# New prices in a planner: product times as traced, one transfer rate for all stages, and a short time for products with 32 stationary columns

## The chip, the cores and the metric

The kernel runs on one core of one Trainium2 chip. The metric is device time in microseconds (us) of one execution. The core has five engines that each work through their own instructions in a fixed order and wait for each other by semaphores: TensorE (PE, matrix products and transposes), VectorE (DVE), ScalarE (ACT), GpSimd (POOL) and SyncE (SP, which here only issues transfers). POOL issues transfers too. All transfers share 16 DMA engines.

## The reference

Two networks follow each other on 256 tokens of width 1024. The first has four layers, each a mixer and a SwiGLU FFN of width 2816; the mixers are a forgetting attention ("fox"), an S5 layer, a pooling layer, and fox again. The second has two layers with a hybrid mixer (retention, latent attention, mLSTM); the first has an FFN of width 2816, the second a mixture of 8 experts of width 3584, of which each token takes two.

```python
def first_block(x, ...):
    for i in range(DEPTH):                       # 4
        h = rms_norm(x, mix_norm_g[i])
        kind, j = i % N_MIXERS, i // N_MIXERS
        if kind == 0:   mix = forgetting_attention(h, fox_w_in[j], fox_b_f[j], fox_w_out[j])
        elif kind == 1: mix = s5_layer(h, s5_w_in[j], ...)
        else:           mix = multiscale_pool(h, pool_w[j], ...)
        x = x + mix
        x = x + swiglu(rms_norm(x, ffn_norm_g[i]), ffn_w_gate_up[i], ffn_w_down[i])
    return rms_norm(x, final_norm_g)

def second_block(x, ...):
    for l in range(DEPTH_2):                     # 2
        mix = hybrid_mixer(x, ...)
        x = layer_norm(DN_ALPHA * x + mix, ln1_w[l], ln1_b[l])
        f = swiglu_2(x, ...) if l % 2 == 0 else moe_swiglu(x, ...)
        x = layer_norm(DN_ALPHA * x + f, ln2_w[l], ln2_b[l])
    return x
```

The S5 layer computes u = h @ w_in, runs a complex linear recurrence over the 256 positions for each of 64 groups of 16 channels, and passes the result through a gated product with w_glu.

## The kernel before

**Products.** All is fp32. A product with a weight matrix is done with three products of a shorter type (fp32r): each weight tile of 128 rows and up to 1024 columns is loaded into a `raw` tile, ACT rounds it to `hi` (or scales and rounds it), DVE computes the rest `lo` (the split), and the activations have the same two parts `xh` and `xl`. The three are hi with xh, lo with xh, hi with xl, each in pieces of 512 columns: PE rows like `ps<-hi,xh`. The weight is loaded as the moving side, 512 columns at a time; the stationary side is the transposed activation of 128 tokens. There are 9 `raw` tiles (four of them are used by the S5 preparation until it ends) and 8 pairs of `hi` and `lo`. SP issues the weight loads, at most as far ahead as `raw` tiles are free.

**Stages.** An FFN goes through its width in blocks of 512 columns of gate and up, the last one of 256. Within a block all products of the first 128 tokens (t=0) come first, then those of t=1. At the end of each, ACT takes the silu of the gate and DVE multiplies it with up; the tail (`tail` in `ffn`) then transposes the result on PE, four 128x128 transposes (`ps<-ident,blk`, line L344), for the products with the down matrix.

**The S5 layer.** `s5_prep` computes the layer's tables (E, rot, T, G) from its parameters. It is started at the beginning and runs on DVE, ACT and PE between the other work of the first fox layer and its FFN. It loads the parameters in two halves with small loads on SP (`in_s_b_re`, `in_s_b_im`, `in_s_c_re`, `in_s_c_im`), and writes the tables to HBM by POOL. `s5` starts with `load`, which fetches the tables back, by POOL, as blocks of 128x512: 20 blocks ahead where the preparation has been planned to its end by then, else 11. The input product `gemm` comes next on PE; its result is scaled with the norm's rstd. In `rstd` a small product with a permutation matrix (loaded from `in_steps`) puts the two rstd vectors into the order of the layer (`ps<-rstd,blk`); the evacuation of the input product (`evac_u`) waits for that. rstd itself ends with a power on POOL (`rstd<-rstd,mhalf`), one for each 128 tokens. Four cores (`core(b)`) then do 16 products of 32 stationary columns each with the E table, the recurrence on DVE, and products with the T and G tables.

**What sets the order.** The class `Net` is a planner that runs while the program is built. It keeps a clock and a planned end for each engine, for the transfers and for each tile. Each piece of side work (a tail, the S5 preparation, a core, a norm) is a generator that sleeps until the planned time at which its data are there; `until` runs all generators that are due before the next product is put down. So the planned times decide where in PE's row each transposition or small product stands, and with it the order on the other engines. On the chip each engine then keeps that order, whatever the real times are. Products are priced in `mm` (L334 to L339), those of the MoE part with 64 stationary columns in `mm_cols` (L331), transposes in `tr` (L344, 0.107 us). Transfers are priced by their bytes over `rate`; `moe` sets `rate` to 395e3 (bytes per us) for its own stage already. An issue on POOL is planned at 1.04 us. Where the planner sees PE wait for 1.2 us or more, `reach` puts filler products of the identity with itself there (L287, planned at 0.214 us each); in the trace each is two rows.

Line L102 is the wrapper through which all instructions of DVE, ACT, POOL and SP pass, so their rows have that line.

Of the kernel before, what the change touches and what calls it, by code (L numbers as in the profile page):

```python
# [11 lines left out]
F32R = mybir.dt.float32r  # L12
# [103 lines left out]
class Net:  # L116
# [1 line left out]
    KEEP = 8  # L118
    BLK = 33
    AHEAD = 2.0  # L120
    rate = 358e3
    HYB = "ambr"
    BW = 528

# [208 lines left out]
    def mm(self, out, lhsT, rhs, start=True, stop=True):  # L333
        n = 1  # L334
        for d in rhs.shape[1:]:
            n *= d
        c = max(n * 0.4219, 107) / 1e3 if lhsT.dtype == F32R else max(n * 1.667, 214) / 1e3
        self.pe(out, (lhsT, rhs), c)
        self.nc.tensor.matmul(out, lhsT, rhs, start=start, stop=stop)  # L339

# [2416 lines left out]
```

## Time and profile before

| | us |
|---|---|
| three runs | 2611.97, 2620.14, 2619.58 |
| median | 2619.58 |
| the profiled execution | 2619.74 |
| its span in the trace | 2617.9 |
| PE busy | 2548.8 |
| mean granted clock of PE | 0.992 |

The trace times below count from the start of the span. The stages are, in us: first fox layer to 147, its FFN to 364, S5 layer from there to about 455, then the FFN of the S5 layer, the pooling layer, its FFN, the second fox layer and its FFN to about 1190, the two hybrid layers with an FFN between them to 1700, and the MoE part to the end. In a timeline a row can stand for several like instructions (x2, x4); its first number is the start of the first, the second the time from there to the end of the last, and a bracket gives the idle time of the engine before it and what ended it. Rows of products overlap, since a product is counted from its entry to its end.

### The profile page before, as it was taken

To read this page: it belongs to the slowest core of one execution; us is meant where nothing else is said; L and a number is where in the kernel's file an instruction comes from. 1 tells how busy PE (TensorE), PEld (TensorE's weight loads), DVE (VectorE), ACT (ScalarE), POOL (GpSimd) and SP (SyncE) were. 2 spreads that over 40 slices of the span, in tenths; PEclk is the share of its full clock that TensorE was granted. 3 is DMA by queue.
4 is the path that set the end of the run, shared out by engine and by line. 5 is a ranking of instruction groups with operands and counts; after the bars stand their busy time and mean duration, and the time that the engine had idled before them with its cause. 6 is when DMAs were issued, how large, how long until landed. Compare 5 with 4: busy or idle time off the path is not lost. (4 is left out here: it accounts for less than half of the span.)

```text
span 2617.9 us, 37366 instructions
## 1 busy us (share of the span) xinstructions
PE 2548.8 (97%) x12588; PEld 1959.1 (75%) x12588; DVE 1719.0 (66%) x2714; ACT 1294.3 (49%) x1829; POOL 130.7 (5%) x222
## 2 busy tenths in 40 slices
PE   8999999999999999999999999999999999999997
PEld 7887776788887888888878878886378883588852
DVE  6798776555655567556785467895088971498921
ACT  5644433454345455443644436484077760487820
POOL 2001034000000000000010010100000000000000
PEclk9999999999999999999999999999999999999999
DMA  6546778556355444564355643799999989999997
GB/s 222 155 153 215 246 256 283 169 165 231 115 189 191 146 138 149 174 209 144 113 191 167 208 141 113 228 373 356 404 386 397 375 309 365 398 395 388 388 368 310
DMA packets 307958, 649.35 MB, mean 248 GB/s; under 512 B 56746, under 2 KB 70408, under 8 KB 307760
## 3 DMA queue, kind: packets, MB, share of 16 engines
q1 hardware_dynamic: 294928, 608.23, 65.9%
q0 software_dynamic: 12640, 38.58, 4.5%
q8 instruction: 101, 1.65, 0.3%
q14 instruction: 97, 0.79, 0.1%
q10 hardware_dynamic: 192, 0.08, 0.0%
HBM read 635.29 MB, written 15.68 MB: 249 GB/s over the span
## 5 line engine op out<-in xcount | busy, mean ns | idle before, releaser
L339 PE MATMUL ps<-hi,blk 128*128 128x512 f32 x3024 | 844.6, 396 | 3.2 <-ACT hi L102 2.8
L102 DVE TENSOR_TENSOR lo<-raw,hi 128x1024 fp32r<-128x1024 f32 (+2 forms) x498 | 565.0, 1158 | 184.2 <-ACT hi L102 174.4
L339 PEld LDWEIGHTS ps<-hi,blk 128*128 128x128 f32 x3024 | 563.8, 189 | 133.6 <-ACT hi L102 5.1
L102 ACT CAST hi<-raw 128x1024 fp32r<-128x1024 f32 (+2 forms) x498 | 487.8, 1000 | 255.0 <-PE ps L339 209.9
L339 PE MATMUL ps<-lo,blk 128*128 128x512 f32 x1512 | 478.9, 395 | 1.1 <-DVE lo L102 1.1
L339 PE MATMUL ps<-lo,xh 128*128 128x512 f32 (+2 forms) x1296 | 418.5, 390 | 2.6 <-DVE lo L102 2.6
L339 PE MATMUL ps<-hi,xh 128*128 128x512 f32 (+2 forms) x1296 | 419.6, 390 | 1.0 <-ACT xh L102 0.9
L339 PE MATMUL ps<-hi,xl 128*128 128x512 f32 (+2 forms) x1296 | 417.7, 389 | 1.0 <-DVE xl L102 1.0
L102 DVE SCALAR_TENSOR_TENSOR lo<-raw,gam,hi 128x1024 fp32r<-128x1024 f32 (+3 forms) x272 | 303.0, 1134 | 81.1 <-ACT hi L102 69.3
L339 PEld LDWEIGHTS ps<-lo,blk 128*128 128x128 f32 x1512 | 282.8, 188 | 64.7 <-DVE lo L102 2.4
L102 ACT ACTIVATE hi<-raw,gam 128x1024 fp32r<-128x1024 f32 (+3 forms) x272 | 275.8, 1031 | 92.9 <-PE ps L339 73.6
L102 DVE TENSOR_TENSOR blk<-ps,blk 128x512 f32<-128x512 f32 (+4 forms) x220 | 139.5, 640 | 273.4 <-PE ps L331 140.7
L339 PEld LDWEIGHTS ps<-hi,xl 128*128 128x128 f32 x1296 | 241.1, 188 | 48.7 <-DVE xl L102 2.0
L339 PEld LDWEIGHTS ps<-lo,xh 128*128 128x128 f32 x1296 | 239.3, 189 | 50.2 <-DVE lo L102 4.7
L339 PEld LDWEIGHTS ps<-hi,xh 128*128 128x128 f32 x1296 | 239.5, 189 | 48.5 <-issue 2.2
L344 PE MATMUL ps<-ident,blk 128*128 128x128 f32 (+3 forms) x957 | 153.0, 278 | 16.1 <-DVE blk L102 12.8
L344 PEld LDWEIGHTS ps<-ident,blk 128*128 128x128 f32 (+3 forms) x957 | 110.6, 137 | 75.0 <-DVE blk L102 44.0
L102 ACT CAST blk<-ps 128x512 fp32r<-128x512 f32 (+2 forms) x137 | 76.2, 556 | 163.7 <-PE ps L344 109.7
L339 PE MATMUL ps<-blk 128*128 128x64 f32 (+11 forms) x1104 | 144.3, 304 | 5.2 <-DVE blk L102 3.1
L339 PEld LDWEIGHTS ps<-blk 128*128 128x128 f32 (+5 forms) x1104 | 118.7, 174 | 28.2 <-ACT blk L102 7.0
L102 ACT ACTIVATE blk<-ps 128x512 f32<-128x512 f32 (+1 forms) x75 | 41.8, 558 | 196.8 <-PE ps L331 135.4
L102 DVE TENSOR_TENSOR lo<-blk,hi 128x512 fp32r<-128x512 f32 x206 | 129.6, 683 | 0.5
(277 smaller groups left out, 1879.8 us busy)
## 6 DMA issues: line engine op xcount, KB each, us to landing
raw<-in_ffn_w_gate_up SPq DMA_DIRECT2D x320, 256.0 KB, 4.4
raw<-in_ffn_w_down SPq DMA_DIRECT2D x110, 512.0 KB, 4.9
raw<-in_moe_w_down SPq DMA_DIRECT2D x109, 512.0 KB, 7.0
raw<-in_moe_w_gate SPq DMA_DIRECT2D x101, 512.0 KB, 7.8
raw<-in_moe_w_up SPq DMA_DIRECT2D x99, 512.0 KB, 8.0
blk<-in_moe_w_up SPq DMA_DIRECT2D x98, 256.0 KB, 7.2
blk<-in_moe_w_gate SPq DMA_DIRECT2D x92, 256.0 KB, 7.8
blk<-in_moe_w_down SPq DMA_DIRECT2D x88, 256.0 KB, 6.6
```

Of the source, the lines that this page charges most:

```text
L102: return real(*a, **k)
L339: self.nc.tensor.matmul(out, lhsT, rhs, start=start, stop=stop)
L344: self.nc.tensor.transpose(out, in_, self.c["ident"][:p, :p])
```

## The change

Three constants of the planner change: the rate of transfers outside the MoE stage, the price of fp32r products (512 columns: 226.7 instead of 216.0 ns), and that of fp32 products (32 stationary columns with over 64 moving ones: 80 ns instead of 214 for 128 columns and 427 for 256; others 13.3 or 8 ns more). No product, split, load or wait is added or removed by hand; only the fillers change in number, from 152 to 157. Below the edit, all later lines have numbers higher by 6, so L339 is L345 and L344 is L350.

```diff
@@ class Net
-    rate = 358e3
+    rate = 395e3
@@ def mm
-        c = max(n * 0.4219, 107) / 1e3 if lhsT.dtype == F32R else max(n * 1.667, 214) / 1e3
+        if lhsT.dtype == F32R:
+            c = max(n * 0.4167 + 13.3, 113) / 1e3
+        elif lhsT.shape[-1] == 32 and n > 64:
+
+            c = 0.08
+        else:
+            c = max(n * 1.667 + 13.3, 222) / 1e3
         self.pe(out, (lhsT, rhs), c)
```

What the new prices do to the order is seen best at three places.

SP's queue in the first FFN, the kernel before: the 80 slices of the 512-wide blocks (gate and up of 8 weight tiles for each of five blocks), then those of the 256-wide block, with the S5 layer's small loads between them.

```order
L102 DMA raw<-in_ffn_w_gate_up 128x512 x80
L102 DMA raw<-in_ffn_w_gate_up 128x256 x10
L102 DMA blk<-in_s_b_re 64x32x16 x2
L102 DMA blk<-in_s_b_im 64x32x16 x2
L102 DMA blk<-in_s_c_re 128x4x64
L102 DMA blk<-in_s_c_im 128x4x64 x2
L102 DMA blk<-in_s_c_re 128x4x64
L102 DMA raw<-in_ffn_w_gate_up 128x256 x6
```

The same place on SP in the changed kernel.

```order
L102 DMA raw<-in_ffn_w_gate_up 128x512 x74
L102 DMA blk<-in_s_b_re 64x32x16 x2
L102 DMA blk<-in_s_b_im 64x32x16 x2
L102 DMA blk<-in_s_c_re 128x4x64
L102 DMA blk<-in_s_c_im 128x4x64 x2
L102 DMA blk<-in_s_c_re 128x4x64
L102 DMA raw<-in_ffn_w_gate_up 128x512 x6
L102 DMA raw<-in_ffn_w_gate_up 128x256 x16
```

The small loads stood ahead of the last six slices of the 256-wide block, and now stand ahead of the last six of the block before it. The preparation's last transposes move on PE from the S5 input product into the first FFN, 129 weight products earlier.

POOL between the end of the S5 preparation and the second norm's power, the kernel before; `s5E<-blk` and the like write tables to HBM, `blk<-s5E` and the like fetch them, and the two `rstd` rows are the powers of the first and the second 128 tokens.

```order
L102 TENSOR_TENSOR rstd_3486<-rstd_3486,mhalf 128x1
L102 DMA s5E<-blk 128x512
L102 DMA blk<-in_steps 128x512
L102 DMA blk<-s5E 128x512 x4
L102 DMA blk<-s5rot 64x512 x4
L102 DMA blk<-s5T 128x512 x4
L102 DMA s5E<-blk 128x512
L102 TENSOR_TENSOR rstd_3663<-rstd_3663,mhalf 128x1
```

The same on POOL in the changed kernel.

```order
L102 TENSOR_TENSOR rstd_3567<-rstd_3567,mhalf 128x1
L102 DMA blk<-in_steps 128x512
L102 DMA blk<-s5E 128x512 x4
L102 DMA blk<-s5rot 64x512 x4
L102 DMA blk<-s5T 128x512 x4
L102 DMA blk<-s5G 128x512 x4
L102 DMA blk<-s5E 128x512 x4
L102 DMA blk<-s5rot 64x512 x4
L102 TENSOR_TENSOR rstd_3764<-rstd_3764,mhalf 128x1
```

24 table loads (20 blocks, since two of `s5rot` make one) instead of 12 stand ahead of the second power.

PE where that power is used, the kernel before, in the S5 input product.

```order
L344 MATMUL ps<-ident,blk 128x128 x4
L339 MATMUL ps<-rstd_3486,blk 128x1
L339 MATMUL ps<-rstd_3663,blk 128x1
L339 MATMUL ps<-rstd_3486,blk 128x1
L339 MATMUL ps<-rstd_3663,blk 128x1
L339 MATMUL ps<-hi,xl_3465 128x512
```

The same on PE in the changed kernel.

```order
L345 MATMUL ps<-hi,xl_3548 128x512 x2
L287 MATMUL ps<-ident 128x128 x18
L345 MATMUL ps<-rstd_3567,blk 128x1
L345 MATMUL ps<-rstd_3764,blk 128x1
L345 MATMUL ps<-rstd_3567,blk 128x1
L345 MATMUL ps<-rstd_3764,blk 128x1
L345 MATMUL ps<-hi,xh_3549 128x512 x2
```

18 fillers now stand ahead of it; it is 48 products into the input product, in both nearly the same place.

PE in the FFN of the S5 layer at the transposes of a t=1 tail, the kernel before.

```order
L339 MATMUL ps<-hi,xl_4561 128x512 x2
L339 MATMUL ps<-hi,xh_4560 128x512 x2
L344 MATMUL ps<-ident,blk 128x128 x4
L339 MATMUL ps<-lo,xh_4560 128x512 x2
L339 MATMUL ps<-hi,xl_4561 128x512 x2
```

The same tail in the changed kernel.

```order
L345 MATMUL ps<-hi,xl_4583 128x512 x2
L345 MATMUL ps<-hi,xh_4582 128x512
L350 MATMUL ps<-ident,blk 128x128 x4
L345 MATMUL ps<-hi,xh_4582 128x512
L345 MATMUL ps<-lo,xh_4582 128x512 x2
```

The four transposes stand one product earlier; the same holds for four tails in each of four FFNs.

## Rows read from the trace of the kernel before

**Rows 1.** The page's first part: busy time, share of the span, instructions

```profile
PE 2548.8 (97%) x12588; PEld 1959.1 (75%) x12588; DVE 1719.0 (66%) x2714; ACT 1294.3 (49%) x1829; POOL 130.7 (5%) x222
```

**Rows 2.** Windows: stretch, length, busy time of each engine, granted clock, DMA share, GB/s

```profile
147.00:274.00 127.00, 126.61 (x594) 98.10 (x593) 111.84 (x189) 57.67 (x67) 18.69 (x31) 1.00 0.65 199
...
1700.00:2618.00 918.00, 891.24 (x4198) 613.17 (x4196) 576.67 (x688) 485.62 (x634) 3.29 (x6) 0.99 0.98 372
1832.00:1898.00 66.00, 65.22 (x346) 25.86 (x345) 4.43 (x9) 5.26 (x10) 0.00 (x0) 1.00 1.03 404
...
398.00:446.00 48.00, 43.43 (x378) 31.23 (x376) 29.81 (x45) 12.81 (x18) 23.96 (x45) 0.89 0.99 342
```

**Rows 3.** PE's groups by form: name, sizes, count, busy, mean ns, idle before

```profile
L287 PE MATMUL ps<-ident 128*128 128x128 f32 x304 | 41.1, 290 | 0.0
...
L339 PE MATMUL ps<-blk,raw 128*32 128x256 f32 x64 | 10.0, 391 | 0.3 <-DVE blk L102 0.2
...
L339 PE MATMUL ps<-blk 128*32 128x128 f32 x256 | 9.7, 293 | 2.3 <-DVE blk L102 2.3
```

**Rows 4.** Timeline of PE at a t=1 tail of the second FFN

```profile
515.04 0.62 PE L339 MATMUL ps<-hi,xh 128*128 128x512 f32 x2
...
516.40 0.61 PE L339 MATMUL ps<-hi,xh 128*128 128x512 f32 x2
517.08 0.66 PE L344 MATMUL ps<-ident,blk 128*128 128x128 f32 x4
```

**Rows 5.** SP's issues in the first FFN

```profile
252.35 3.83 SPq L102 DMA_DIRECT2D blk<-in_s_b_re  x2
...
267.80 4.10 SPq L102 DMA_DIRECT2D raw<-in_ffn_w_gate_up  x6
```

**Rows 6.** Timeline of ACT ahead of the stall at 275

```profile
272.14 0.72 ACT L102 ACTIVATE hi<-raw,gam 128x512 fp32r<-128x512 f32 x1 [3.15 <-DMA raw<-in_ffn_w_gate_up]
```

**Rows 7.** Timeline of PE at that stall

```profile
274.84 0.39 PE L339 MATMUL ps<-hi,xh 128*128 128x512 f32 x1
278.62 1.11 PE L344 MATMUL ps<-ident,blk 128*128 128x128 f32 x4 [3.39 <-DVE blk L102]
```

**Rows 8.** Windows of 4 us behind it, columns as in rows 2

```profile
278.00:282.00 4.00, 3.38 (x10) 2.90 (x11) 3.65 (x6) 0.59 (x1) 0.00 (x0) 0.50 1.00 401
282.00:286.00 4.00, 4.00 (x16) 3.20 (x15) 1.38 (x2) 0.59 (x1) 0.54 (x1) 0.72 0.16 63
```

**Rows 9.** Timeline of PE at the way into the S5 layer

```profile
364.16 2.17 PE L287 MATMUL ps<-ident 128*128 128x128 f32 x18
368.82 0.65 PE L344 MATMUL ps<-ident,blk 128*128 128x128 f32 x4 [2.49 <-DVE blk L102]
...
370.91 1.20 PE L339 MATMUL ps<-hi,xh 128*128 128x512 f32 x2
...
382.26 0.95 PE L339 MATMUL ps<-rstd,blk 128*128 128x1 f32 x8
```

**Rows 10.** Timeline of DVE there

```profile
362.57 4.87 DVE L102 SCALAR_TENSOR_TENSOR lo<-raw,gam,hi 128x1024 fp32r<-128x1024 f32 x4
```

**Rows 11.** Timeline of POOL there

```profile
359.92 2.16 POOL L102 DMA_DIRECT2D blk<-s5E  x4
...
365.29 0.57 POOL L102 DMA_DIRECT2D blk<-s5T  x1 [0.62 <-DMA blk<-s5E]
367.42 0.54 POOL L102 DMA_DIRECT2D blk<-s5T  x1 [1.56 <-DMA blk<-s5E]
368.85 0.54 POOL L102 DMA_DIRECT2D blk<-s5T  x1 [0.89 <-DMA blk<-s5E]
...
374.17 0.56 POOL L102 TENSOR_TENSOR rstd<-rstd,mhalf 128x1 f32<-128x1 f32 x1 [2.57 <-DVE rstd L102]
```

**Rows 12.** Timeline of all engines at the end of the first fox layer

```profile
150.02 1.28 DVE L102 TENSOR_TENSOR x<-ps,x 128x512 f32<-128x512 f32 x2
...
151.01 0.60 PE L344 MATMUL ps<-ident,x 128*128 128x128 f32 x4
```

## The prediction

> **What bounds the kernel now.** I read the busy shares first: TensorE (PE) is busy 97% of the span [rows 1]. Then the busy time stage by stage: up to 1700 us PE has no long holes and the transfers have room, while the MoE stage (1700 to 2618) keeps the 16 DMA engines busy 98% of the time at 372 GB/s [rows 2]. So in the first 1700 us a change in the order of the instructions can only win or lose where PE stands still, runs at a lower clock, or runs fillers; and what it wins or loses there moves the whole MoE stage by as much. I then looked for those places in the timelines: the tail of every FFN block [rows 4], the stall at 275 [rows 5 to 8], and the way into the S5 layer at 364 [rows 9 to 11].
>
> PE does the same products before and after. The change alters only the prices by which the planner decides who stands before whom, so everything below is about order.
>
> **The prices.** Six consecutive 512-column products start 1.36 us apart from the first to the seventh, 0.227 us each [rows 4]: the new 226.7 ns is right, the old 216.0 was 5% short. The products with 32 stationary columns come in two kinds: the S5 cores' 16 products of 128 columns, and two of 256 columns in the S5 preparation. The profile's means (293 and 391 ns, overlapping neighbours included) differ by 98 ns [rows 3], so one price of 80 ns cannot be right for both; it is the wide kind that it prices too low. The new rate of 395 GB/s for all stages is met in a stretch of pure weight loading (404 GB/s) and not where the S5 tables are loaded (342 GB/s at a DMA share of 0.99) [rows 2].
>
> The Trainium skill's page "DMA: Bandwidth & Descriptors", section Bandwidth, speaks against the new rate: for traffic between HBM and SBUF it says that "the HBM side (~358) binds". The 404 GB/s of this trace are above that, so the rule does not hold for long weight rows here; the 342 of the S5 stage are below it. By that rule every load of the first 1700 us would be planned about a tenth too early, which is the third rival below.
>
> **Part by part.** Every product is planned longer, so planned data arrive after fewer planned products: things that wait for data move a little ahead on PE.
>
> 1. FFN tails. In each of the four 11-block FFNs, the second half of the tail transposes moves exactly one product forward in four blocks, 16 in all. They already wait: after the two products at 516.40 the next could start at 516.85, and the transposes start at 517.08 [rows 4]. What they wait for does not come sooner, so the product that stood ahead now stands behind: 16 x 0.227 = +3.6 us. Bounds: 0 if the evacuation is early enough, 3.6. The row shows a wait, so I take 3.6.
>
> 2. fox layers. At the end of the first one, the transposes of the second x tile move 14 products forward, with two fillers ahead. Before, they start at 151.01, about when the first half of the add (150.02, 1.28 for both) is done [rows 12]: no slack. VectorE is busy 112 of 127 us there [rows 2], so the add comes little sooner. Bounds 0 and 14 x 0.227 = 3.2; I take +2. In the second fox layer the heads move up to 12 products forward: 0 to 2.7, I take +1.5.
>
> 3. Fillers (L287: products of the identity with itself which the planner puts where it thinks that PE waits). 304 rows are 152 of them, and 41.1 us [rows 3], so 0.27 us each. The hybrid layers lose 8: -2.2. The pool layer loses 4: -1.1. The router's change by few, in front of waits.
>
> 4. The stall at 275. PE waits 3.39 us for transposes of the S5 preparation [rows 7], VectorE behind ScalarE, ScalarE 3.15 us for weights [rows 6]; after having stood still PE runs 4 us at a granted 0.50 (1.2 of its 2.4 GHz) and 4 at a mean of 0.72 [rows 8], which loses 2.0 + 1.1 us. The cause is on SP's queue: from 252.35 to 267.80 it was held by the small S5 loads, and the last six weight slices of the block stood behind them [rows 5]. From there to the first product that needs those slices there were 70 products (counted in the order) x 0.227 = 15.9 us, less than the 15.4 of the queue plus landing and split. After the change the same S5 loads stand one block earlier, and the first product that needs the slices behind them is 91 products, 20.7 us away. I take the stall as gone: 3.39 + 3.1 = -6.5. Bounds: -6.5 and 0 (late again in the new place).
>
> 5. The way into S5. Before, nine fillers end at 366.3 and the first S5 product starts at 370.91; PE waits 2.49 us for a transpose of the S5 preparation that stands ahead of those of x [rows 9]. VectorE had four lo splits (4.87 us) [rows 10] and steps of the S5 preparation ahead of the x adds. After, the S5 preparation has ended 129 products earlier and three splits remain: one split (1.22) falls away, and with the S5 steps the wait of 2.49 for them. Bounds -4.6 (from 366.3 to 370.91) and 0; I take -3, nearer to the 3.7 that these two make.
>
> 6. The S5 norm. This is the new wait. The product of rstd with a permutation (`rstd,blk`) stands in the middle of the S5 input product, behind 18 new fillers. It needs the second rstd, which POOL computes behind its table loads: 12 before, 24 now. Before, POOL issued 8 at about 0.54 us each, then was held back to one per 2.13 us (365.29 to 367.42) or 1.43 us (to 368.85), and had rstd at 374.17, long before PE asked for it at 382.26 [rows 9, 11]. Now the first eight are issued by about 364, and after them stand 16 loads, 12 of 256 KB and 4 of half that, so 14 times that pace: 14 x 1.43 = 20.0, rstd at 384.6; at 2.13, 394. PE gets to the place after 48 products, at 368 + 10.9 + 1 = 380, and has done its fillers (18 x 0.24, by the nine at 364.16 in 2.17) at 384.3. The fillers alone cost 4.3; with POOL at 384.6 and the hop to PE, +6.5; with 394, +14. The later rows of POOL show the shorter pace, so +6.5; bounds 4.3 and 14.
>
> 7. S5 cores. 20 table blocks instead of 10 are fetched ahead. PE is idle 4.57 us in the stage 398 to 446 [rows 2]; I take -3, bounds +6 and -4.5.
>
> 8. VectorE's lag. With S5 work packed tighter into the first FFN, where VectorE is nearly full [rows 2], evacuations come later: 0 to 5, I take +2.5.
>
> 9. MoE. Tails move as in item 1, but the transfers set the end there [rows 2]; 0 to 3.9 (17 x 0.227), I take +1.5.
>
> Sum: 3.6 + 2 + 1.5 - 2.2 - 1.1 - 6.5 - 3 + 6.5 - 3 + 2.5 + 1.5 = +1.8 us. The profiled execution took 2619.74, which is the median of the runs (2619.58) within 0.2, so the forecast is 2621.5.
>
> **The rivals.**
>
> - Faster. The S5 region keeps its gains and rstd is there when the fillers end: tails and fox at half (1.8 + 1), fillers -3.3, stall -6.5, entry -4, norm +4.3, cores -3, lag 0, MoE 0: -9.7, about 2610. For it: all the large gains are waits read from rows. Against it: VectorE is nearly full, and it is behind the entry as well.
> - Slower. POOL's rstd waits behind the 24 loads at the slow pace. The weight loads run at the same time, and the DMA engines are full in this stage; that is what held POOL back before. Norm +14 and, as tables and weights share the same transfers, no gain in the cores: 1.8 + 7.5 + 3 = +12.3, about 2632. It decides from a rstd later than about 388 on the clock of before. Against it: the two last intervals on POOL were 1.4.
> - The change does not do what it says: transfers priced at 395 that move at 342 in the S5 stage. 48 us of transfers at 342 are planned as 48 x 342 / 395 = 41.6, so tables may come up to 6.4 us later than planned, and the cores' gain of 3 falls away: 1.8 + 6.4 + 3 = +11.2, about 2631. This is also what the page's rule would do, here as a mechanism of this kernel. Against it: more tables are fetched ahead than before.
>
> **How the numbers follow.** A measurement of this kernel can tell about 0.3%, 7.9 us, from no change. Chances: my sum 0.48, faster 0.22, slower by POOL 0.20, slower by transfers 0.10. Most of the sum's own spread (+-6) lies within 0.3%. Faster by over 0.3%: most of the second case and a little of the first, 0.22. Slower by over 0.3%: the last two and a little of the first, 0.32. Within: 0.46. The range takes in the faster case with its stall bound (2607) and the norm at its dear end with a late table (2636).
>
> **What would show it.** Right: in the new trace no wait of PE on VectorE in the first FFN's last block; 18 fillers and a wait of one to three us ahead of `rstd,blk`, with POOL's second rstd after its table loads; the S5 entry without a transpose of the preparation; tails of the FFNs waiting about 0.45 instead of 0.22. Wrong: a wait on weights one block earlier in the first FFN, a POOL pace that is not the DMA queue's, cores that wait for tables, or an end of the MoE stage that does not follow its start.

## The result

| | before | changed |
|---|---|---|
| median of the runs, us | 2618.72 (2611.97 to 2620.14, 4 runs) | 2648.08 (2646.68 to 2650.77, 4 runs) |
| profiled execution, us | 2619.74 | 2646.98 |
| its span, us | 2617.9 | 2645.2 |

The changed kernel is slower: ratio 1.0119, 95% interval 1.0107 to 1.0131, 29 us. The forecast was 2621.5 with a range of 2607 to 2636. The sign was right by 1.8 us only, and the time lies 12 us outside the range. In the later comparisons, of 9 to 13 runs each, the kernel before took 2615.9 us.

### The profile after

The first part of the page of the changed kernel answers to [rows 1]: PE is busy 14.1 us more, of which 2.4 us are fillers (314 rows, 43.5 us, in the groups by form; before 304 and 41.1). The other 13 us of the longer span are idle time of PE.

```profile
PE 2562.9 (97%) x12598; PEld 1966.3 (74%) x12598; DVE 1726.2 (65%) x2725; ACT 1290.5 (49%) x1818; POOL 130.9 (5%) x222
```

The fillers' row, from the groups of PE by form, answers to the first of [rows 3].

```profile
L287 PE MATMUL ps<-ident 128*128 128x128 f32 x314 | 43.5, 296 | 0.0
```

Both traces have 8916 weight products (rows of PE that read `hi` or `lo` beside activations), and up to the MoE part they stand in one order, so the n-th is the same product in both, and its start in the one trace less that in the other tells where time went. This table is made from the starts in the two timelines; "to product" is the number of the first product behind the stretch, counted from 0.

| stretch of PE's work | to product | start there before, us | lost (+) or won (-) in it, us | my term |
|---|---|---|---|---|
| start and input products of the first fox layer | 336 | 102.9 | +2.6 | 0 |
| its heads and output product, with the first 24 products of the FFN | 456 | 153.3 | +10.1 | +2 |
| its FFN, to the end of the fourth block | 816 | 246.2 | +5.3 | +2.5 |
| the fifth and the last block, with the stall | 960 | 292.9 | -0.8 | -6.5 |
| the down product and entry to the S5 layer | 1224 | 370.9 | -1.4 | -3 |
| S5 norm and cores | 1440 | 471.3 | -1.0 | +3.5 |
| FFN of the S5 layer | 2300 | 680.8 | +1.3 | +0.9 |
| pooling layer, its FFN, second fox layer and its FFN | 4420 | 1230.4 | +3.1 | +2.2 |
| first hybrid layer | 4800 | 1362.5 | +3.7 | -1.1 |
| the FFN behind it | 5440 | 1513.9 | +0.8 | +0.9 |
| second hybrid layer | 5976 | 1706.2 | +3.9 | -1.1 |
| MoE | 8915 | 2602.7 | -0.3 | +1.5 |

So three places that I had priced at about zero or as a gain made most of it: the first fox layer (+10.1), the hybrid layers (+7.6 together) and the first FFN, whose stall came back in its new place.

Each kernel has one trace. Four later runs keep the changed kernel's order on PE over long parts (m1_fill, m3_hybrid_old, m4_tail_later, n2_fill_early, below), and where they keep it they show how far a stretch can be trusted. The start lies between +2.6 and +5.1, the heads between +10.1 and +11.5 (in m3_hybrid_old and m4_tail_later, which leave them alone), the S5 norm and cores between -1.0 and +4.8, the MoE part between -2.7 and -0.3; the FFN to its fourth block agrees within 0.2. The start, to which I had given no term, was not followed further.

**The tails, as forecast.** This is the timeline of PE at the tail of [rows 4] in the changed kernel. From the single product at 531.48 the next could start at 531.71; the transposes start at 532.14, so they wait 0.43 us where they waited 0.23. The one product more stands behind them.

```profile
531.02 0.62 PE L345 MATMUL ps<-hi,xl 128*128 128x512 f32 x2
531.48 0.39 PE L345 MATMUL ps<-hi,xh 128*128 128x512 f32 x1
532.14 0.66 PE L350 MATMUL ps<-ident,blk 128*128 128x128 f32 x4 [0.28 <-DVE blk L102]
532.55 0.47 PE L345 MATMUL ps<-hi,xh 128*128 128x512 f32 x1
```

**The S5 norm, as forecast.** Timeline of POOL, then of PE, at the place of [rows 9] and [rows 11]. The second rstd follows the 24 loads at 398.88, which is 383.2 on the clock of before when the 15.7 us lost up to product 1224 are taken off (forecast 384.6). PE is in its 18 fillers then (from 397.64, 4.18 us), and `rstd,blk` stands behind them at 401.66 without a wait. The fillers are the cost, as the lower bound of that term (4.3) had it, not the 6.5 that I took.

```profile
398.88 0.57 POOL L102 TENSOR_TENSOR rstd<-rstd,mhalf 128x1 f32<-128x1 f32 x1
```

```profile
380.49 2.17 PE L287 MATMUL ps<-ident 128*128 128x128 f32 x18
385.54 1.16 PE L350 MATMUL ps<-ident,x 128*128 128x128 f32 x8 [2.88 <-DVE x L102]
397.64 4.18 PE L287 MATMUL ps<-ident 128*128 128x128 f32 x36
401.66 0.95 PE L345 MATMUL ps<-rstd,blk 128*128 128x1 f32 x8
```

The second row there is the entry: no transpose of the S5 preparation stands there any more, but PE waits 2.88 us for the x adds all the same (2.49 before), since VectorE had eight lo splits in one row ahead of them, not the three that I read from the order.

```profile
375.13 9.65 DVE L102 SCALAR_TENSOR_TENSOR lo<-raw,gam,hi 128x1024 fp32r<-128x1024 f32 x8 [0.63 <-ACT hi L102]
384.71 1.28 DVE L102 TENSOR_TENSOR x<-ps,x 128x512 f32<-128x512 f32 x2
```

**The stall, against the forecast.** The rows of SP, ACT and PE that answer to [rows 5], [rows 6] and [rows 7]. SP is held by the small loads from 244.76 to 261.34, 16.6 us; ACT waits 4.70 and 1.92 us for weights; PE waits 4.46 us. What PE waits for are the four transposes of an FFN tail, the one of the block before: ACT's silu (270.14) stands behind the rounding that waited for weights, and DVE's multiplication (271.47) behind that slice's split.

```profile
244.76 9.00 SPq L102 DMA_DIRECT2D blk<-in_s_b_re  x2
...
261.34 28.87 SPq L102 DMA_DIRECT2D raw<-in_ffn_w_gate_up  x22
```

```profile
265.54 1.15 ACT L102 ACTIVATE hi<-raw,gam 128x1024 fp32r<-128x1024 f32 x1 [4.70 <-DMA raw<-in_ffn_w_gate_up]
...
269.09 1.15 ACT L102 ACTIVATE hi<-raw,gam 128x1024 fp32r<-128x1024 f32 x1 [1.92 <-DMA raw<-in_ffn_w_gate_up]
270.14 0.67 ACT L102 ACTIVATE blk<-ps,rstd 128x512 f32<-128x512 f32 x1
```

```profile
270.27 1.28 DVE L102 SCALAR_TENSOR_TENSOR lo<-raw,gam,hi 128x1024 fp32r<-128x1024 f32 x1 [2.26 <-ACT hi L102]
271.47 0.74 DVE L102 SCALAR_TENSOR_TENSOR blk<-ps,rstd,blk 128x512 f32<-128x512 f32 x1
```

```profile
272.27 1.11 PE L350 MATMUL ps<-ident,blk 128*128 128x128 f32 x4 [4.46 <-DVE blk L102]
```

It was the same before, in the timelines of ACT and then of DVE ahead of the transposes of [rows 7].

```profile
276.39 0.72 ACT L102 ACTIVATE hi<-raw,gam 128x512 fp32r<-128x512 f32 x1 [1.71 <-DMA raw<-in_ffn_w_gate_up]
277.02 0.67 ACT L102 ACTIVATE blk<-ps,rstd 128x512 f32<-128x512 f32 x1
```

```profile
277.81 0.75 DVE L102 SCALAR_TENSOR_TENSOR blk<-ps,rstd,blk 128x512 f32<-128x512 f32 x1
```

**The first fox layer, not foreseen.** Timeline of PE at the end of its heads, waits alone, then windows of 4 us (stretch, length, busy time of PE, PEld, DVE, ACT, POOL, granted clock, DMA share, GB/s). PE stands still for 1.7 us in three waits between 127.8 and 130.8, mostly behind the maximum of the softmax (`mx`) on DVE, and then runs three windows at a granted 0.50 (1.2 GHz). In the kernel before the waits there are 0.95, 0.32 and 0.17, and the clock stays at 1.00; its rows and windows follow those of the changed kernel.

```profile
128.93 0.52 PE L350 MATMUL ps<-ident,blk 128*128 128x128 f32 x3 [1.16 <-DVE mx L102]
129.67 0.82 PE L350 MATMUL ps<-ident,blk 128*128 128x128 f32 x3 [0.23 <-DVE mx L102]
...
130.84 2.00 PE L345 MATMUL ps<-blk 128*128 128x64 f32 x12 [0.34 <-DVE blk L102]
```

```profile
128.00:132.00 4.00, 2.42 (x16) 1.81 (x16) 3.93 (x16) 1.86 (x8) 0.00 (x0) 0.97 0.00 0
132.00:136.00 4.00, 4.00 (x18) 3.82 (x19) 3.28 (x10) 0.74 (x2) 1.24 (x2) 0.50 0.31 67
136.00:140.00 4.00, 3.90 (x15) 2.75 (x14) 0.98 (x6) 2.38 (x10) 0.00 (x0) 0.50 0.22 65
140.00:144.00 4.00, 4.00 (x17) 3.71 (x17) 3.79 (x18) 1.64 (x3) 1.18 (x2) 0.50 0.21 45
```

```profile
126.39 0.55 PE L344 MATMUL ps<-ident,blk 128*128 128x128 f32 x3 [0.95 <-ACT blk L102]
...
130.04 0.66 PE L344 MATMUL ps<-ident,blk 128*128 128x128 f32 x4 [0.32 <-DVE blk L102]
...
131.81 0.44 PE L344 MATMUL ps<-ident,blk 128*128 128x128 f32 x2 [0.17 <-ACT blk L102]
```

```profile
124.00:128.00 4.00, 3.04 (x22) 2.46 (x20) 1.49 (x2) 4.00 (x9) 0.00 (x0) 1.00 0.00 0
128.00:132.00 4.00, 3.52 (x25) 2.66 (x23) 2.99 (x10) 1.72 (x7) 0.00 (x0) 1.00 0.79 244
132.00:136.00 4.00, 3.97 (x23) 3.14 (x22) 3.60 (x13) 1.53 (x6) 0.00 (x0) 1.00 0.07 25
```

The order on PE tells why. Counted in it, 54 small products and transposes of the heads stand between the products 336 and 376 in the kernel before and 46 up to 400; in the changed kernel it is 25 and then 75, of which 13 stand directly ahead of product 376 (a product that is two rows in the trace counts once; the expectation below says 74, which was a slip). The theory is that the heads fall behind the weight products, and that at the end there are too few weight products left to fill PE while the last softmax is worked out.

### The profile page after: what moved, and what is told of

The parts are those of the page before. It is cut to its first block, busy times and chain, and to the rows that moved or that the text cites. A ratio compares the mean times of both kernels' runs of the same rounds, so it can differ in the third digit from the quotient of the medians.

```text
span 2645.2 us, 37419 instructions
## 1 busy us (share of the span) xinstructions
PE 2562.9 (97%) x12598; PEld 1966.3 (74%) x12598; DVE 1726.2 (65%) x2725; ACT 1290.5 (49%) x1818; POOL 130.9 (5%) x222
## 5 line engine op out<-in xcount | busy, mean ns | idle before, releaser
L345 PE MATMUL ps<-hi,blk 128*128 128x512 f32 x3024 | 847.7, 396 | 6.1 <-ACT blk L102 2.3
L345 PEld LDWEIGHTS ps<-hi,blk 128*128 128x128 f32 x3024 | 563.3, 189 | 136.7 <-issue 4.5
L345 PE MATMUL ps<-lo,blk 128*128 128x512 f32 x1512 | 477.8, 395 | 1.1 <-DVE lo L102 1.1
L345 PE MATMUL ps<-hi,xh 128*128 128x512 f32 (+2 forms) x1296 | 422.6, 391 | 2.4 <-ACT xh L102 1.5
L345 PE MATMUL ps<-lo,xh 128*128 128x512 f32 (+2 forms) x1296 | 416.1, 387 | 1.9 <-DVE lo L102 1.9
L345 PE MATMUL ps<-hi,xl 128*128 128x512 f32 (+2 forms) x1296 | 416.9, 388 | 0.7 <-DVE xl L102 0.7
L345 PEld LDWEIGHTS ps<-lo,blk 128*128 128x128 f32 x1512 | 283.8, 188 | 64.6 <-DVE lo L102 1.9
L102 DVE TENSOR_TENSOR blk<-ps,blk 128x512 f32<-128x512 f32 (+3 forms) x220 | 140.0, 641 | 281.1 <-PE ps L331 138.4
L345 PEld LDWEIGHTS ps<-lo,xh 128*128 128x128 f32 x1296 | 240.8, 188 | 50.3 <-DVE lo L102 3.0
L345 PEld LDWEIGHTS ps<-hi,xl 128*128 128x128 f32 x1296 | 240.6, 188 | 49.3 <-issue 3.0
L345 PEld LDWEIGHTS ps<-hi,xh 128*128 128x128 f32 x1296 | 238.4, 189 | 47.9 <-ACT xh L102 2.6
L350 PE MATMUL ps<-ident,blk 128*128 128x128 f32 (+3 forms) x957 | 154.6, 281 | 20.9 <-DVE blk L102 16.9
L350 PEld LDWEIGHTS ps<-ident,blk 128*128 128x128 f32 (+3 forms) x957 | 110.3, 138 | 83.4 <-DVE blk L102 48.3
L345 PE MATMUL ps<-blk 128*128 128x64 f32 (+10 forms) x1104 | 150.8, 308 | 5.7 <-DVE blk L102 2.6
L345 PEld LDWEIGHTS ps<-blk 128*128 128x128 f32 (+5 forms) x1104 | 125.9, 181 | 29.8 <-issue 9.5
```

What stands on the lines that cost most here:

```text
L102: return real(*a, **k)
L350: self.nc.tensor.transpose(out, in_, self.c["ident"][:p, :p])
```

## The experiments

Theory: the planner's order is what costs; wherever side work (heads, S5 preparation, mixers, tails) changes its place among the weight products, PE waits for VectorE or ScalarE, and the fp32r price moves nearly all of it. Rivals: the higher transfer rate makes weights late; the short price for 32 columns disturbs the S5 layer and its preparation; or it is the clock alone.

### One price at a time

Each edit is made alone in the kernel before.

```diff
 e1_rate
-    rate = 358e3
+    rate = 395e3
 e2_f32r
-            c = max(n * 0.4219, 107) / 1e3
+            c = max(n * 0.4167 + 13.3, 113) / 1e3
 e3_col32
+        elif lhsT.shape[-1] == 32 and n > 64:
+            c = 0.08
 e4_fp32
-            c = max(n * 1.667, 214) / 1e3
+            c = max(n * 1.667 + 13.3, 222) / 1e3
```

> Only the transfer rate is changed (395e3 for all stages); all product prices are those of before. Theory (the product price of fp32r made the loss): the order on PE is that of before nearly everywhere, so the time is that of before within 8 us (ratio 0.997 to 1.003). Rival (transfers are planned too early at 395 and weights come late): slower by 10 to 29 us (ratio 1.004 to 1.011), with PE waiting on ScalarE or DMA in the first FFN and the S5 stage.

> Only the price of fp32r products is changed (226.7 instead of 216.0 ns for 512 columns); rate and fp32 prices are those of before. Theory: nearly the whole loss, +20 to +30 us (ratio 1.0076 to 1.0115): about +10 at the end of the first fox layer, +5 in its FFN, +4 in each hybrid layer, +3.6 in the tails of the FFNs. Rival (rate or the short price for 32 columns made it): +4 to +8 us, the tails alone.

> Only the price of products with 32 stationary columns is changed (80 ns). The order differs from before only from the middle of the first FFN to the S5 cores. Theory: between -6 and +6 us, from the stall at 275 us and the S5 stage alone. Rival (the preparation's products, priced too short, make VectorE's side work late): +10 us or more, all of it in the first FFN.

> Only the price of the other fp32 products is changed (8 to 13 ns more each). The order differs in the fox layers, the S5 stage and the hybrid layers. Theory: between -5 and +8 us. Rival (attention products, which are fp32, made the loss in the fox and hybrid layers): +10 to +20 us.

| kernel | median, us | before beside it | ratio, 95% interval |
|---|---|---|---|
| e1_rate | 2617.73 | 2615.99 | 1.0007 (0.9998 to 1.0017) |
| e2_f32r | 2640.86 | 2615.99 | 1.0100 (1.0081 to 1.0119) |
| e3_col32 | 2631.51 | 2615.99 | 1.0063 (1.0044 to 1.0081) |
| e4_fp32 | 2652.21 | 2615.99 | 1.0135 (1.0118 to 1.0152) |

In the medians the rate costs nothing that can be told from noise, so the rival of late transfers falls as the cause of the 29 us. Its one trace is not that of before, though: the profiled execution was the longest of its ten (2623.15 us), it gained 5.0 us in the blocks with the stall (products 816 to 960) and lost 7.6 in the S5 cores (1224 to 1392, granted clock 0.82 where before has 0.93), which is the place and about the size that the transfer rival of the prediction named (6.4). In the changed kernel and the four traces that keep its order there the stretch stands between -1.5 and +4.3, so the rival does not explain the 29 us; what it is worth in e1_rate alone stays open.

The fp32r price alone makes 25 us. But the theory as I had written it was too narrow: the two small prices were expected at within 8 us and cost 15 and 36. The four do not add up to the whole (1.7 + 24.9 + 15.5 + 36.2 = 78 against 29), so there is no price that "is" the loss. Each is a shift of the order, and each of the three product prices ends with a worse order than that of before. For the price of 32 columns alone the rival holds: most of its loss lies in the S5 stage. The changed kernel has that price too, and there its stage moved by -1.0.

In e4_fp32 the loss in the first FFN is large (14.6 us between the products 528 and 660; most of the rest lies in the two hybrid layers, 6.2 and 7.4), and its timeline shows a second form of the same thing: steps of the S5 preparation stand on DVE ahead of the lo splits, the planner knows it and has put 27 fillers there, and beside them PE waits for hi and lo. First PE, then DVE.

```profile
178.40 0.73 PE L342 MATMUL ps<-hi,xh 128*128 128x512 f32 x2 [1.09 <-ACT hi L102]
178.97 1.95 PE L287 MATMUL ps<-ident 128*128 128x128 f32 x16
```

```profile
179.72 0.75 DVE L102 TENSOR_TENSOR blk<-raw 128x256 f32<-128x256 f32 x2
...
182.10 1.28 DVE L102 SCALAR_TENSOR_TENSOR lo<-raw,gam,hi 128x1024 fp32r<-128x1024 f32 x1
```

In e3_col32 the stall of [rows 7] has become longer, 8.88 us, with ACT 8.35 us behind the weights; the rest of its loss lies in the S5 stage (+12 us between the products 1224 and 1392), which I did not follow further.

```profile
282.96 1.11 PE L349 MATMUL ps<-ident,blk 128*128 128x128 f32 x4 [8.88 <-DVE blk L102]
```

### The first fox layer: order and clock

The first experiment takes the old product prices for that layer alone; two others add fillers to the changed kernel, and move nothing else. The edits are shortened: `n.old` makes `mm` use the product prices of before.

```diff
 n1_fox0_old
+        n.old = True            # mm: prices of before
         n.fox(0, n.res_add)
+        n.old = False
 m1_fill (in tr; FILL = {128: 5, 131: 1})      n2_fill_early (FILL = {127: 5, 130: 1, 133: 2})
         self.pe(out, (in_,), 0.107)
+        self.n_tr += 1
+        for _ in range(FILL.get(self.n_tr, 0)):
+            self.nc.tensor.matmul(out, ident, ident, start=True, stop=True)
```

> The changed kernel with the product prices of before in the first fox layer only; the heads stand among the weight products as before there (54 small products and transposes between weight products 336 and 376, 46 up to 400, against 25 and 74). Theory (the heads fall behind the weight products, and at the end PE has none left to do while ACT and DVE do the softmax): the stretch from 336 to 456 is as long as before, 10 us less than the changed kernel. Rival (the loss comes from the rate and the weights, or from the S5 preparation beside it): more than half of the 10 us stays. What comes later is planned from another state, so the total may differ by more than that.

> The changed kernel with six more fillers on PE at the end of the first fox layer, five ahead of the transposes that wait 1.16 us at 128.93 and one ahead of those that wait at 129.67; nothing else moves. Theory (half of the loss at that place is the clock: PE stood still for 2 us and then ran at a granted 0.50 from 132 to 144): the clock stays at 1.00 and the stretch to weight product 456 gets 5 to 6 us shorter, so 2642 to 2643 us. Rival (order alone, and the clock fell for something else): the same 2648 or 1 us more, clock still 0.50.

> The changed kernel with eight fillers at the end of the first fox layer, five of them ahead of the last transpose that does not wait, so that PE works through most of the 1.16 us in which it stood still at 127.8. Theory (the low clock is worth about 5 of the 10 us there, since the kernel with the fp32r price alone has the same small products in the same stretches, kept 1.00 and lost 4.7): the clock stays at 1.00 and the stretch to 456 is 4 to 5 us shorter than in the changed kernel. Rival (while the clock is low, PE waits on ACT and DVE anyway): 0 to 1 us, with more waits instead.

n1_fox0_old took 2634.69 us (before beside it 2615.92; ratio 1.0072, 1.0057 to 1.0087). From product 336 to 456 it is as long as before within 0.1 us: the 10.1 us come from the order of the heads, which the product prices set. (Its FFN is then planned from another state, with 14 fillers and 11.3 us lost between 528 and 660, so not all of it is kept.)

m1_fill took 2648.77 us (ratio to before 1.0133, 1.0116 to 1.0150): nothing gained. Its fillers were written to the PSUM bank of the transposes that wait, and the timeline shows that they waited as well, 1.06 us, though they read nothing but the identity: so it is the bank, which DVE's maximum must give free, that the transposes wait for, and not their own data; the clock fell one window later (0.86 from 136 to 140, 0.50 to 144), and the stretch got 1.0 us shorter, which is within the spread of this stretch (10.1 to 11.5).

```profile
128.98 1.38 PE L353 MATMUL ps<-ident 128*128 128x128 f32 x10 [1.06 <-DVE mx L102]
```

n2_fill_early took 2644.71 us (ratio 1.0120, 1.0104 to 1.0135). Here five of eight fillers go to the bank of a transpose that does not wait, and they run in the 1.16 us. The clock stays at 1.00 in all windows to 164, and the stretch from 336 to 456 is 4.2 us shorter than in the changed kernel (+5.9 instead of +10.1), as expected. So the low clock is worth 4.2 of the 10.1 us. The other 5.9 remain at full clock: PE stands still for 2.9 us in the stretch (before 1.5) and runs ten fillers, about 2.5 us at 0.25 each; what is left was not taken apart. The median over the whole is 3.4 us under that of the changed kernel, but in different comparisons, and the ratios to before are the same (1.0120 and 1.0119), so the gain is shown by the stretch alone.

```profile
127.83 1.25 PE L353 MATMUL ps<-ident 128*66 128x128 f32 x10
```

```profile
132.00:136.00 4.00, 3.83 (x28) 2.99 (x27) 3.93 (x12) 0.52 (x2) 1.25 (x2) 1.00 0.20 43
136.00:140.00 4.00, 3.13 (x19) 2.25 (x19) 2.27 (x8) 4.00 (x12) 0.00 (x0) 1.00 0.35 92
```

e2_f32r says the same from another side: it has as many small products in the same stretches as the changed kernel (25 and 75), its clock stayed at 1.00, and it lost 4.7 us there. PE's waits add up to 3.1 us in its stretch and to 3.0 in the changed kernel's, so their sum does not tell which of the two falls to the low clock.

### The hybrid layers

The edit is shortened in the same way.

```diff
 m3_hybrid_old (the same for hybrid(1))
+        n.old = True
         n.hybrid(0, (n.ln_res, lambda: aff(1, 0)))
+        n.old = False
```

> The changed kernel with the product prices of before in the two hybrid layers only; up to the first of them the order is that of the changed kernel. Theory (the loss in the hybrid layers comes from side work that now stands too early on PE and waits for VectorE): 6 to 8 us less than the changed kernel, 2640 to 2642. Rival (it comes from a shifted start of these layers, or from transfers): no more than 2 us less.

2640.29 us (ratio to before 1.0091, 1.0072 to 1.0111), 7.8 less than the changed kernel in another comparison; m1_fill, which is the changed kernel with six fillers more, took 2648.77 in the same one. The first hybrid layer now loses 0.1 us instead of 3.7 and the second 1.6 instead of 3.9, so 5.9 us come from these layers. Most of the rest lies in the MoE part (-3.3 instead of -0.3), which has the order of before again; among the traces with that order this part differs by over 4 us, so the rest is no result. The loss is waiting: PE's waits in the first hybrid layer add up to 7.3 us in the changed kernel and 3.6 before, in the second to 10.7 and 7.0. Three of them in the first, within 4 us:

```profile
1343.18 0.66 PE L350 MATMUL ps<-ident,blk 128*128 128x128 f32 x4 [1.25 <-DVE blk L102]
1344.51 0.73 PE L345 MATMUL ps<-hi,blk 128*128 128x512 f32 x2 [0.68 <-ACT blk L102]
1346.43 1.20 PE L345 MATMUL ps<-hi,blk 128*128 128x512 f32 x4 [0.73 <-DVE blk L102]
```

Eight fillers had fallen away in these layers, which I had booked as a gain of 2.2 us. The granted clock is 1.00 in both kernels in the first of them and 0.98 in both in the second, so it is not the clock that the missing fillers cost. m3_hybrid_old brings back six of them and the old order together, so it does not part the two.

### The stall in the first FFN

The S5 preparation's second set of small loads is issued by POOL instead of SP in the kernel before; the planner still books it on SP, so no other instruction moves. Lines between those shown are left out.

```diff
 m2_s5_on_pool (get in s5_prep)
+        pool = Eng(self, "sync", nc._nc.gpsimd)
+            q_ = pool if h else nc.sync
-                    nc.sync.dma_start(z[q].rearrange("p (g c) -> p g c", c=16)[64 * (i ^ q):64 * (i ^ q) + 64], src)
+                    q_.dma_start(z[q].rearrange("p (g c) -> p g c", c=16)[64 * (i ^ q):64 * (i ^ q) + 64], src)
-                    nc.sync.dma_start(rv[:, :, x_], A[nm][0, h * 32:h * 32 + 32].rearrange("(k g) c p -> (g c) k p", k=4))
+                    q_.dma_start(rv[:, :, x_], A[nm][0, h * 32:h * 32 + 32].rearrange("(k g) c p -> (g c) k p", k=4))
```

> The kernel before, with the S5 preparation's second set of small loads issued by POOL instead of SP (planned as before, so no other instruction moves). Theory (the stall at 275 comes from SP's queue being held for 15.4 us by these loads): the wait of 3.39 us and the low clock after it are gone, 4 to 7 us faster, 2609 to 2612. Rival (the many small packets fill the DMA engines, whoever issues them): weights are as late as before, no change within 2 us.

2612.08 us against 2615.85, ratio 0.9988 (0.9979 to 0.9998). Between the products 816 and 960 its trace is 5.5 us shorter than that of before. The timelines of POOL, SP and PE: POOL issues the eight loads within 7.4 us (258.84 to 266.19), SP goes through the 22 slices without a break, and PE's wait is 1.53 us instead of 3.39; the granted clock in the windows of [rows 8] is 1.00. So the move is worth 3.8 us in the medians, as the theory had it and not the rival. That the held queue made the whole stall of the trace of before is not shown, however. In e1_rate PE, ACT, DVE and SP have the order of before there, the same small loads hold SP's queue for 15.1 us (252.61 to 267.72), and yet PE waits 1.00 us, less than the 1.53 here, the granted clock stays at 1.00 and the stretch is 5.0 us shorter than before. The six slices behind the loads landed by 274.1 there and by 276.3 in the trace of before, and ACT's last rounding ahead of the silu did not wait for them (274.28, against 276.39 after a wait of 1.71). So the same held queue gives a short or a long wait, as the slices behind it happen to land, and the 3.39 us with the low clock behind them are a long one.

```profile
258.84 2.21 POOL L102 DMA_DIRECT2D blk<-in_s_b_re  x2
261.03 2.17 POOL L102 DMA_DIRECT2D blk<-in_s_b_im  x2
...
266.19 1.10 POOL L102 DMA_DIRECT2D s5E<-blk  x2
```

```profile
237.61 31.36 SPq L102 DMA_DIRECT2D raw<-in_ffn_w_gate_up  x22
269.08 29.77 SPq L102 DMA_DIRECT2D raw<-in_ffn_w_down  x13
```

```profile
277.28 0.66 PE L344 MATMUL ps<-ident,blk 128*128 128x128 f32 x4 [1.53 <-DVE blk L102]
```

The same row of PE in e1_rate, with SP's queue held as before:

```profile
276.50 0.66 PE L347 MATMUL ps<-ident,blk 128*128 128x128 f32 x4 [1.00 <-DVE blk L102]
```

### The tails, and a kernel that is faster than both

```diff
 m4_tail_later (in the changed kernel, 0.23), b1 (0.23) and b2 (0.46) (in m2_s5_on_pool)
-                    yield self.at(h)
+                    yield At(self.when(h) + self.tail_late)    # in ffn's tail; 0 in the first FFN
```

> The changed kernel with the tails of the FFNs after the first planned 0.23 us later, which puts every one of them one product back: those of t=1 to where they stood before, those of t=0 one product later than before. Theory (a tail that waits costs what it stands too early): -3.7 us for t=1 and up to -2.5 for t=0, whose transposes wait 0.14 us, so 2642 to 2645. Rival (the products that follow fill the wait): no change within 1 us in the FFNs.

> The kernel before with the second set of small S5 loads on POOL, and with the tails of the FFNs after the first planned 0.23 us later, which puts each of them one product back. Theory: -4 from the loads, -2.5 to -6 from the tails (20 of each kind wait 0.14 and 0.22 us before): 2606 to 2610 against 2616. Rival (the tails' transposes cost more in their new place, or the end of the MoE stage takes it back): no better than the loads alone, 2612.

> The same with the tails planned 0.46 us later, two products back. Theory: the waits at the tails are gone in both kinds, 1 to 2 us less than with one product, 2605 to 2609. Rival: nothing left to gain, and the last tail of each FFN comes too late for the down product, 1 to 3 us more than with one product.

m4_tail_later took 2644.12 us (ratio to before 1.0106, 1.0089 to 1.0123), 4.0 less than the changed kernel in another comparison. In the FFN of the S5 layer, product 1440 to 2300, it stands at -1.0 against before where the changed kernel has +1.3, and the other FFNs gain 1 to 2 us each; its profiled execution stands at +4.8 in the S5 norm and cores, where nothing was changed and the changed kernel has -1.0, so its total tells less than the FFNs' own stretches.

b1_pool_tail23 took 2606.14 us, ratio 0.9964 (0.9951 to 0.9978), and b2_pool_tail46 2603.03, ratio 0.9952 (0.9939 to 0.9966), both against 2615.92 for the kernel before. The first fell into its range (2606 to 2610); the second came out 2 us below its own (2605 to 2609) and is faster than both kernels of this case, by 13 us in its own comparison and by 45 across two. The timeline of PE in b2_pool_tail46 at the tail of [rows 4], which now stands two products later, shows no wait: two products start at 510.87, the next could start 2 x 0.227 later, and the transposes start just then, at 511.33.

```profile
510.87 0.62 PE L340 MATMUL ps<-lo,xh 128*128 128x512 f32 x2
511.33 0.60 PE L345 MATMUL ps<-ident,blk 128*128 128x128 f32 x4
```

## Why the prediction was wrong

**Right: the prices and the tails.** The fp32r price is what PE does, and 16 tails moved by one product cost about what the working says, 4 x 0.23 = 0.9 in each FFN: +1.3 in the FFN of the S5 layer and +0.8 in the one behind the first hybrid layer. What was lost before the MoE stage (27.5 us) reached the end almost whole (27.3), as the prediction had it. The true price made the kernel slower at this place, because the old price, 5% too short, had put the tails nearer to where their data were.

**Right: the S5 norm and cores as a whole.** Rstd came at 383.2 on the clock of before (384.6 forecast), 18 fillers cost 4.2 us, and the slow POOL rival did not come. The stage from 1224 to 1440 moved by -1.0, where the terms together say +3.5; in the other four traces with this order it stands between 0.0 and +4.8, so the sum is not refuted here, and not measured closely either.

**Wrong: item 2, the first fox layer.** The term was +2, measured +10.1, and it failed in what was looked at. I followed the transposes of x at the end of the layer and priced the heads of the second fox layer, and did not count how the heads of the first stand among the weight products. They went from 54 and 46 small products to 25 and 75, the opposite of the "move a little ahead" that I had put over all parts. Two terms came out of it: 5.9 us at full clock, with waits behind the softmax and fillers among them, and 4.2 us because PE, having stood still for 1.7 us, ran at half clock. The granted clock of 1.00 in the profile before did not say that it would stay so in the new order.

**Wrong: item 4, the stall.** The step that failed is the path. I counted the products up to the first that reads the late slices (91, 20.7 us) and took PE to be free until then. But what PE stops for is a tail, both before and after (I had read the transposes of [rows 7] as those of the S5 preparation): its silu on ACT and its multiplication on DVE stand behind the rounding and the split of the late slices. So PE stops at product 831, 15 products ahead of the first that reads them (846, counted in the order), and starts again 10.9 us after the queue is free (272.27 less 261.34). I had also set the 15.4 us of the queue against the 20.7 without the landing and the split that the same item counts for the place before. What I had as the dear bound, "late again in the new place", is what happened: -0.8 instead of -6.5. And the 6.5 themselves were the size of one execution, as e1_rate shows.

**Wrong: item 3, the fillers.** I took fillers that go away as pure gain, which they are only where PE has other work at that moment. In the hybrid layers the side work had moved and PE waits 3.7 us more in each: +7.6 instead of -2.2, and old prices there take 5.9 back. How much of it the fillers themselves make is not shown.

**Mis-sized: items 5 and 8.** The entry to S5 with the down product gave 1.4 us instead of 3: VectorE had eight splits in one row, so the x adds came as late as before. VectorE's lag in the first FFN was +5.3 instead of +2.5, just over the bound of 5. Only 1.2 us of it are waits of PE on VectorE; about 2.3 are work of the preparation that stands earlier, 60 transposes in this stretch instead of 36, four of which take 0.38 us. The rest was not found.

**The rivals.** None was what happened. The transfers at 395 GB/s fall as a cause of the 29 us with e1_rate (1.7 us, not distinguishable from nothing), though its one trace lost 7.6 us in the S5 cores. The rule of the Trainium skill's page "DMA: Bandwidth & Descriptors", section Bandwidth, which speaks against the rate, did not decide the time here; the stretch of 404 GB/s in the trace of before stands against it, and in the changed kernel the MoE stage ran at 369 GB/s, as before at 372.

**The range** left out that several terms could come out dear together. As I read it, they had a common cause: a price moves all side work at once, in a kernel in which VectorE is nearly full where the side work is. The sum treated eleven places as if each had its own luck. Its lower end, 2607, does not follow from the working either: the faster case has the stall at its bound already and gives 2610.

## What to carry to other kernels

In a program whose order is made from planned times, a truer price is a new order and not a better one: go through each stage where side work runs beside the main products and count how it is distributed among them before and after, first where the engine that feeds it is nearly full. A wait that is read from the trace can be had without touching the prices: move the transfer to another queue, or the waiting instruction back by the time that it waits; both together made this kernel 13 us faster, while each of the three product prices alone made it slower.

## What had not been expected of the hardware

- PE stood still for 1.7 us in 3 and then ran at a granted 0.50 for three windows of 4 us. With eight fillers, five of them (1.25 us) ahead of the wait and to a bank that was free, it stayed at 1.00 and the stretch was 4.2 us shorter; with six, five of them to the bank of the waiting transposes, those five waited too, the clock fell one window later, and the stretch was 1.0 shorter, within its spread.
- The same eight small loads held SP's queue for 15.4 and 16.6 us, and the weights behind them; issued by POOL they took 7.4 us of POOL, and SP did not stop. Behind a queue held as long (15.1 us in e1_rate) PE waited 1.00 us instead of 3.39.
